# Three block-Winograd stages: combinations of the second input half traced in pieces, and two weight splits queued behind the scaled transposes

## The chip, the cores and the metric

One core of one Trainium2 chip runs the whole program. The metric is the device time of one execution in microseconds, as the median of several runs. The engines are TensorE (PE in the profile; PEld are its weight loads), VectorE (DVE), ScalarE (ACT), GpSimd (POOL) and SyncE (SP), which here issues the plain loads.

## The reference

Two layers work on 512 tokens of width 1024. Each has a token mixer and a squared-ReLU MLP, each behind an RMSNorm and added to the residual.

```
for i in range(DEPTH):                       # DEPTH = 2
    h = rms_norm(x, norm_mix[i])
    x = x + (mla_mixer(h, ...) if i % 2 == 0 else chunked_sgu_mixer(h, ...))
    h = rms_norm(x, norm_ffn[i])
    x = x + jnp.square(jax.nn.relu(h @ w_up[i])) @ w_down[i]    # 1024 -> 4096 -> 1024
return rms_norm(x, final_norm)
# chunked_sgu_mixer: gelu(h @ w_in), 1024 -> 4096; half of it normalised, mixed in chunks and
# used as a gate for the other half; then @ w_out, 2048 -> 1024
```

The change touches the first product of three stages: `h @ w_up` of layer 0 (called FFN0 here), `h @ w_in` (SGU) and `h @ w_up` of layer 1 (FFN1).

## The kernel before

**Arithmetic.** All products are in float32. Each operand is split into two parts of lower precision, high = round(a) and low = a - high, and a product is three matmuls: high by high, high by low, low by high (`mm3`, L110). `split` makes the two parts of a tile: a copy on ACT (L125), then a subtraction on DVE (L122). A tile of weights is 128 x 2048; an input quarter 128 x 1024.

**Seven products for eight.** Large products are taken by a Strassen-Winograd scheme with seven block products. The input, transposed, has four quarters a11, a21 (first half of the columns, ready early) and a12, a22 (second half). The class `Quarters` makes them. `first` turns the first half and gives A11 and S3. `rest` makes what the other five products need: A12; n1 = a22 - a21 and N1; s2 = -n1 - a11 and S2; A22; s4 = -a12 - s2 and S4. Capital names are the splits. `turn` (L312) does a half: four times four transposes on PE into a PSUM bank (L296), then one half of the bank scaled on ACT (L316) and the other on DVE (L317).

**Items.** Each stage is a list `work` of items. An item has `prepare` (fetch or combine the weights, then split them) and `go` (48 matmuls of 256 columns in FFN0 and FFN1, 24 of 512 in the gates of SGU, then the handling of the result). The loops at the end of `ffn` and of the SGU stage prepare two items ahead. In FFN0 and FFN1 the items begin: 0 uses A11, 1 uses S3, 2 uses A12, 3 uses S2, 4 uses N1, 5 uses A22, 6 uses S4. In SGU two such lists run side by side: 0 and 1 use A11, 2 and 3 A12, 4 and 5 N1, 6 and 7 S4, 8 and 9 S2, 10 and 11 S3, 12 and 13 A22.

**Weights.** `load` (L987) is a plain load on SP. `add` (L990) is a load issued by POOL that adds to what the tile holds. In FFN0 and FFN1 item 2 loads a tile of its own ("c"). Item 3's weights are made by `p2` (L1044), a DVE addition of tile "b" to tile "a", followed by the split. Item 4's are "b" after an `add`, which can only start when L1044 has read "b". Item 5's are "a" after another `add`, which can only start when item 3's split has read "a". In SGU the weights of items 2 and 3 pass one after the other through one tile, `W`, so the second load waits for the split of the first.

**Order.** The instructions are traced in the order of the Python code. A scheduler then gives each engine a fixed order: when an engine is free in its own model, it takes the earliest-traced instruction that is ready. So an instruction that is traced late can stand in front of one traced early that still waits. On the chip each engine keeps that order. `tc.issue_after(ins)` puts what a block traces on `ins`'s engine behind `ins`, without waiting for its end; `behind(pair)` does so for two instructions. `wtiles` has three slots for split weights.

**Before the change** `rest` runs as a whole inside `go` of item 0. In FFN0 and FFN1 it writes a12, a22 and n1 into tiles of the pool for the squares. In SGU it writes them into `uq[0]`, the tile u0 whose memory later serves as the slots U1 and U2 for the weights of items 6 and 7.

Of the kernel before, what the change touches and what calls it, by code (L numbers as in the profile page):

```python
# [18 lines left out]
T = 512  # L19
# [38 lines left out]
def trunk(ctx: ExitStack, tc: tile.TileContext, a):  # L58
# [65 lines left out]
    def split(hl, src, eng=None):  # L124
        nc.scalar.copy(hl[0], src)  # L125
        low(eng or nc.vector, hl[1], src, hl[0])
        return hl
# [162 lines left out]
    def four(dtype=F32R):  # L290
        return gxp.tile([P, 4, H], dtype, tag="g", name=nm("g"))
# [7 lines left out]
    class Quarters:  # L299
# [12 lines left out]
        def turn(self, e, lo, hi):  # L312
            for k in range(4):
                kk = self.halves[e] * 4 + k
                ps, g = turned(kk), self.g[kk]
                nc.scalar.activation(lo[:, k, :], ps[:, 0:H], AF.Copy, scale=g)  # L316
                nc.vector.tensor_scalar(  # L317
                    out=hi[:, k, :], in0=ps[:, H:T], scalar1=g, scalar2=None, op0=ALU.mult
                )

        def first(self):
# [6 lines left out]

        def rest(self, a12, a22, n1):

            self.turn(1, a12, a22)
            stt = nc.vector.scalar_tensor_tensor
            nc.vector.tensor_sub(n1, a22, self.a21)
            s2, s4 = self.a11, a12
            stt(out=s2, in0=n1, scalar=-1.0, in1=self.a11, op0=ALU.mult, op1=ALU.subtract)
            self.A12 = split((four(), G6[0]), a12)
            stt(out=s4, in0=a12, scalar=-1.0, in1=s2, op0=ALU.mult, op1=ALU.subtract)
            self.S2 = split((G6[1], G6[2]), s2)
            self.N1 = split((G6[3], G6[4]), n1)
            self.A22 = split((G6[5], four()), a22)  # L340
            self.S4 = split((four(), four()), s4)

# [215 lines left out]
    with tc.tile_pool(name="att", bufs=1) as att:  # L560
# [347 lines left out]
        def after(i, u):  # L908
            norm.add(i, u)
# [3 lines left out]
        def go(n):  # L913
            for _ in range(min(n, len(waiting))):
                waiting.pop(0)()
# [76 lines left out]
    def ffn(layer, xq, norm, pool, after=None, last=None, mid=None):  # L992
# [24 lines left out]
        def up(c):  # L1017

            def w(i, k):
                return wview(w_up, xq.row(k), 512, c * 1024 + i * 512, 512)  # L1020

            s, sq, acc = {}, {}, {}
            X, YZ = banks[0:2], banks[2:4]
            acc = {"X": X, "Y": YZ, "Z": YZ if c else banks[4:6]}

            def fetch(name, i, k):
                s[name] = raws.get()
                load(s[name], w(i, k))

            def w11():  # L1030
                fetch("b", 0, 0)
                return "b"

            def w12():
                fetch("c", 0, 1)
                return "c"

            def p1():
                fetch("a", 1, 0)
                add(s["a"], w(1, 1))  # L1040
                return "a"

            def p2():
                nc.vector.tensor_add(s["a"], s["a"], s["b"])  # L1044
                return "a"

            def p3():
                add(s["b"], w(1, 0))
                return "b"

            def p4():
                add(s["a"], w(0, 1))
                return "a"

            def w22():
                fetch("c", 1, 1)
                return "c"

            def both(name, f):
                if name not in sq:  # L1060
                    sq[name] = squares.get()
                for j in range(2):
                    f(sq[name][:, 2 * j : 2 * j + 2, :], j)

            def pv(ps):
                return ps.rearrange("p (m n) -> p m n", m=2)

            def keep(name, sums):
                both(name, lambda t, j: nc.scalar.copy(t, pv(acc[sums][j])))

            def plus(name, sums):
                both(name, lambda t, j: nc.vector.tensor_add(t, t, pv(acc[sums][j])))  # L1072

            def square(name, scale):
                t = sq[name]
                nc.scalar.activation(t, t, AF.Relu, scale=scale)
                nc.scalar.activation(t, t, AF.Square)

            def end1():
                keep("a11", "X")  # L1080

            def end2():
                plus("a11", "Z")
                square("a11", 1.0)

            def end5():
                keep("a22", "Y")

            def end6():
                keep("a21", "X")  # L1090

            def end7():
                plus("a22", "X")
                square("a22", -1.0)

            def end3():
                plus("a21", "Y")
                square("a21", 1.0)

            def end4():  # L1100
                both("a12", lambda t, j: nc.scalar.activation(
                    t, pv(acc["X"][j]), AF.Relu, scale=-1.0))
                nc.scalar.activation(sq["a12"], sq["a12"], AF.Square)

            def item(weights, right, sums, first, end, free=False):
                ww = []

                def prepare():
                    name = weights()
                    ww.extend(split(wtiles(4, 512, 16), s[name]))  # L1110
                    if free:
                        raws.put(s.pop(name))

                def go():
                    r = getattr(xq, right)
                    for m in range(4):
                        ms = slice(m * P, (m + 1) * P)
                        out = acc[sums][m // 2][:, (m % 2) * H : (m % 2 + 1) * H]
                        for k in range(4):
                            mm3(  # L1120
                                out, (ww[0][:, k, ms], ww[1][:, k, ms]),
                                (r[0][:, k, :], r[1][:, k, :]),
                                first and k == 0 and m % 2 == 0, k == 3, skip_group_check=True,
                            )
                    end()

                return prepare, go

            m1 = item(w11, "A11", "X", True, end1)
            m2 = item(w12, "A12", "Z", True, end2, True)  # L1130
            m5 = item(p1, "S3", "Y", True, end5)
            m6 = item(p2, "S2", "X", False, end6)
            m7 = item(p3, "N1", "X", False, end7, True)
            m3 = item(p4, "A22", "Y", False, end3, True)
            m4 = item(w22, "S4", "X", False, end4, True)
            if c == 0:
                begin = m1[1]

                def first():
                    begin()  # L1140
                    three = [squares.get() for _ in range(3)]
                    xq.rest(*three)
                    for t in three:
                        squares.put(t)
                    nc.vector.reciprocal(r2, norm.mean())
                    nc.vector.tensor_scalar(
                        out=nr2, in0=r2, scalar1=-1.0, scalar2=None, op0=ALU.mult
                    )

                return [(m1[0], first), m5, m2, m6, m7, m3, m4], sq  # L1150
            return [m1, m2, m5, m6, m7, m3, m4], sq

        def accumulate(i, u, ps, r):
# [131 lines left out]
        n_mixed = len(work)  # L1285
        if last is None:
            work += down(3, sq)
        ahead = 2
        for prepare, _ in work[:ahead]:
            prepare()  # L1290
        for j, (_, go) in enumerate(work):
            if j == 1:
                spare[:] = banks[6:8]
            if j == 7:
                spare[:] = []
            if j == n_mixed:
                spare[:] = banks[0:2]
            go()
            if j + ahead < len(work):
                work[j + ahead][0]()  # L1300
        if last is not None:
            spare[:] = banks
            last(
# [24 lines left out]
    with stage(1), tc.tile_pool(name="sgu", bufs=1) as sg:  # L1328
# [378 lines left out]
        def after(n, f):  # L1707
            then.setdefault(n, []).append(f)

        def begin():  # L1710
            gx1.rest(*(uq[0][t] for t in ("a11", "a12", "a21")))
            r = inv_sqrt(norm1.mean())
            with tc.issue_after(root[0].ins):
                mix_load()
            norms["r"], norms["nr"] = r, small()
            nc.vector.tensor_scalar(
                out=norms["nr"], in0=r, scalar1=-1.0, scalar2=None, op0=ALU.mult
            )
# [25 lines left out]
        def banks_are(t):  # L1744
            spare[:] = t

        after(0, begin)
        after(6, lambda: banks_are(E))
        after(8, rows_of_r)
        after(9, lambda: (mix_transposed(0), mix_transposed(1)))  # L1750
# [23 lines left out]
        for j, (_, go) in enumerate(work):  # L1774
            go()
            for f in then.get(j, ()):
                f()
            if j + ahead < len(work):
                work[j + ahead][0]()
        fixed[0] = None  # L1780

# [116 lines left out]
```

## Time and profile before

| | us |
|---|---|
| median of 3 runs | 1098.06 (1094.0 to 1098.29) |
| the profiled execution, its own time | 1092.22 |
| span of its instructions | 1090.5 |
| mean granted clock | 0.989 of full speed |

The three stages begin near 177 us (FFN0), 502 us (SGU) and 763 us (FFN1) of the span. The timeline gives, for each engine, the start of an instruction (or of several alike in a row), how long it lasted, and in brackets how long the engine stood idle before it and what ended that. Busy times of matmuls overlap, as they are pipelined; the distance between starts is the cost of one.

### The profile page before, as it was taken

The numbers are of one execution on the slowest core, as the hardware profiler recorded it, in microseconds if no ns is written. First come the engines' busy times: TensorE is split into PE (matmuls) and PEld (weight loads), VectorE is DVE, ScalarE is ACT, GpSimd is POOL, SyncE is SP. The second block draws the span as 40 slices with busy tenths as digits, with TensorE's granted clock in tenths as the row PEclk, the third lists the DMA queues.
The fourth block names the chain that finished last, engine by engine and source line by source line (L and its number), as shares of the span: only waits on it lengthen the run. The fifth ranks groups of instructions, "written<-read, shape, count | busy, mean of one in ns | idle before, by whom it ended". The sixth has DMA issues, their size and how long they took to land.

```text
span 1090.5 us, 15740 instructions
## 1 busy us (share of the span) xinstructions
PE 1058.8 (97%) x6540; PEld 947.4 (87%) x6540; DVE 864.3 (79%) x959; ACT 627.8 (58%) x712; POOL 115.4 (11%) x143
## 2 busy tenths in 40 slices
PE   8989999899999999989999999999999999999997
PEld 6778889899999999877788999887999899999986
DVE  6888866887887887887968588997988788888753
ACT  4567546665655655556755645556765555656531
POOL 5100000001001001002011000010001001001000
PEclk9989999999999999999999999999999999999999
DMA  6120246768768669447486836876686886757421
GB/s 204 39 79 2 76 117 197 204 142 174 212 144 186 178 149 199 149 78 175 139 161 141 231 85 193 237 134 181 156 222 125 218 194 125 225 115 119 120 109 59
DMA packets 86083, 163.33 MB, mean 150 GB/s; under 512 B 4917, under 2 KB 10620, under 8 KB 85884
## 3 DMA queue, kind: packets, MB, share of 16 engines
q0 software_dynamic: 33584, 67.11, 35.3%
q1 hardware_dynamic: 52428, 95.22, 25.4%
q8 instruction: 51, 0.84, 0.3%
q14 instruction: 20, 0.16, 0.0%
HBM read 160.22 MB, written 2.10 MB: 149 GB/s over the span
## 4 chain that ended last, share of the span: by engine, by line
PE 79%; DVE 8%; DMA 4%; issue 4%; ACT 4%; SPq 0%; POOL 0%; POOLq 0%; ACTq 0%; DVEq 0%
PE ps L110 74%; DVE wl L122 3%; ACT wh L125 2%; DMA wb<-in_sgu_w_in 2%; DMA wb<-in_ffn_w_down 1%; DVE g L122 1%; PE ps L1613 1%; PE ps L852 1%; DMA wb<-in_ffn_w_up 1%; PE ps L296 1%; PE ps L819 0%; PE ps L820 0%; PE ps L821 0%; PE ps L823 0%; PE ps L822 0%
## 5 line engine op out<-in xcount | busy, mean ns | idle before, releaser
L110 PE MATMUL ps<-g,wh 128*128 128x256 f32 (+1 forms) x2304 | 420.5, 285 | 9.0 <-DVE g L122 5.0
L110 PEld LDWEIGHTS ps<-g,wh 128*128 128x128 f32 x2304 | 359.9, 190 | 17.2 <-DVE g L122 5.9
L110 PE MATMUL ps<-g,wl 128*128 128x256 f32 (+1 forms) x1152 | 327.1, 284 | 0.6 <-DVE wl L122 0.6
L110 PE MATMUL ps<-wh,q 128*128 128x512 f32 (+1 forms) x840 | 266.5, 390 | 2.9 <-DVE x L1155 2.9
L122 DVE TENSOR_TENSOR wl<-wb,wh 128x2048 fp32r<-128x2048 f32 x75 | 171.7, 2289 | 68.8 <-ACT wh L125 68.8
L110 PEld LDWEIGHTS ps<-g,wl 128*128 128x128 f32 x1152 | 217.4, 189 | 2.2 <-DVE wl L122 0.9
L125 ACT CAST wh<-wb 128x2048 fp32r<-128x2048 f32 x75 | 143.0, 1907 | 119.5 <-PE ps L110 92.0
L110 PEld LDWEIGHTS ps<-wh,q 128*128 128x128 f32 x840 | 158.1, 189 | 34.9 <-issue 3.3
L122 DVE TENSOR_TENSOR wl<-wr,wh 128x2048 fp32r<-128x2048 f32 (+1 forms) x69 | 153.3, 2225 | 38.5 <-ACT wh L125 38.4
L125 ACT CAST wh<-wr 128x2048 fp32r<-128x2048 f32 (+1 forms) x69 | 127.8, 1855 | 64.2 <-PE ps L110 44.8
L110 PE MATMUL ps<-wl,q 128*128 128x512 f32 (+1 forms) x420 | 163.7, 390 | 0.0
L110 PE MATMUL ps<-wh,g 128*128 128x512 f32 x496 | 157.5, 395 | 1.9 <-DVE g L122 1.3
L110 PEld LDWEIGHTS ps<-wh,g 128*128 128x128 f32 x496 | 93.8, 189 | 23.3 <-DVE g L122 1.7
L125 ACT CAST q<-sq 128x1024 fp32r<-128x1024 f32 x51 | 53.6, 1051 | 90.4 <-PE ps L110 87.8
L110 PE MATMUL ps<-wl,g 128*128 128x512 f32 x248 | 97.7, 394 | 1.7 <-DVE wl L122 1.7
L110 PEld LDWEIGHTS ps<-wl,q 128*128 128x128 f32 x420 | 79.5, 189 | 14.5
L1155 DVE SCALAR_TENSOR_TENSOR x<-ps,s,x 128x512 f32<-128x512 f32 x98 | 72.6, 746 | 20.9 <-PE ps L110 20.9
L122 DVE TENSOR_TENSOR q<-sq,q 128x1024 fp32r<-128x1024 f32 x51 | 62.4, 1223 | 5.3 <-ACT q L125 2.3
L110 PEld LDWEIGHTS ps<-wl,g 128*128 128x128 f32 x248 | 46.9, 189 | 12.5 <-DVE wl L122 2.5
L990 POOL DMA_DIRECT2D wr<-in_ffn_w_up x16 | 20.9, 1308 | 268.9 <-DMA wr<-in_ffn_w_up 84.9
L990 POOL DMA_DIRECT2D wb<-in_ffn_w_down x17 | 21.9, 1291 | 133.8 <-DVE wl L122 131.6
L1072 DVE TENSOR_TENSOR sq<-sq,ps 128x512 f32<-128x512 f32 x48 | 32.6, 681 | 3.9 <-PE ps L110 2.6
(267 smaller groups left out, 1276.2 us busy)
## 6 DMA issues: line engine op xcount, KB each, us to landing
wb<-in_ffn_w_up SPq DMA_DIRECT2D x18, 1024.0 KB, 5.7
wb<-in_ffn_w_down SPq DMA_DIRECT2D x18, 1024.0 KB, 5.1
wb<-in_ffn_w_down POOLq DMA_DIRECT2D x17, 1024.0 KB, 9.4
wr<-in_ffn_w_up POOLq DMA_DIRECT2D x16, 1024.0 KB, 8.5
wr<-in_ffn_w_up SPq DMA_DIRECT2D x14, 1024.0 KB, 5.5
wr<-in_sgu_w_in POOLq DMA_DIRECT2D x9, 1024.0 KB, 10.4
wr<-in_ffn_w_down SPq DMA_DIRECT2D x8, 1024.0 KB, 5.1
wb<-in_ffn_w_up POOLq DMA_DIRECT2D x8, 1024.0 KB, 8.6
```

The source lines that it names most:

```text
L110: nc.tensor.matmul(out, lhsT=lhsT, rhs=rhs, start=start and t == 0, stop=stop and t == 2, **kw)
L122: return eng.tensor_sub(l, src, h.bitcast(F32))
L125: nc.scalar.copy(hl[0], src)
L296: nc.tensor.transpose(ps[:, i * P : (i + 1) * P], x[:, i, k * P : (k + 1) * P], ident)
L852: nc.tensor.transpose(ps[b][:, c : c + P], pr[h, i][:, j * P : (j + 1) * P], ident)
L990: nc.gpsimd.dma_start(t, src, accum_op=ALU.add)
L1072: both(name, lambda t, j: nc.vector.tensor_add(t, t, pv(acc[sums][j])))
L1155: nc.vector.scalar_tensor_tensor(out=xs, in0=ps, scalar=r[:, i : i + 1], in1=xs, op0=ALU.mult, op1=ALU.add)
L1613: nc.tensor.matmul(ps[:, i * P : (i + 1) * P], lhsT=m[:, i, :], rhs=wt[:, j // 2, :], start=True, stop=True,)
```

## The change

It makes `rest` return six functions instead of doing the work, and calls them in the loops after the `go` of certain items:

| piece | FFN0 and FFN1: traced after | SGU: traced after |
|---|---|---|
| `second`: the transposes, scaling, A12 | item 0 | item 0 |
| `difference`: n1 | item 1 | item 0 |
| `sums`: s2, S2 | item 1 | item 3 |
| `negative`: N1 | item 2 | item 0 |
| `both_sums`: s4 | item 3 | item 3 |
| `others`: A22 and S4 | item 3, A22 first | item 3, S4 first |

`turn` keeps its last pair of scalings in `self.ends`, and in all three stages the `prepare` of items 2 and 3 runs inside `behind(...ends)`: all that it traces on ACT and DVE goes behind the last scaling of that engine. In FFN0 and FFN1 the small scalings of the norm move from item 0 to after item 2. In SGU the three tiles are now the two halves of `Bt` and `wt`, which are not filled until items 9 and 10; u0 is no longer used for them.

```diff
+                self.ends = (
+                    nc.scalar.activation(lo[:, k, :], ps[:, 0:H], AF.Copy, scale=g),
+                    nc.vector.tensor_scalar(
+                        out=hi[:, k, :], in0=ps[:, H:T], scalar1=g, scalar2=None, op0=ALU.mult
+                    ),
                 )
...
+            def second():
+                self.turn(1, a12, a22)
+                self.A12 = split((four(), G6[0]), a12)
+            def difference():
+                nc.vector.tensor_sub(n1, a22, self.a21)
+            def sums():
+                stt(out=s2, in0=n1, scalar=-1.0, in1=self.a11, op0=ALU.mult, op1=ALU.subtract)
+                self.S2 = split((G6[1], G6[2]), s2)
+            def negative():
+                self.N1 = split((G6[3], G6[4]), n1)
+            def both_sums():
+                stt(out=s4, in0=a12, scalar=-1.0, in1=s2, op0=ALU.mult, op1=ALU.subtract)
...
+        then = {
+            0: [begin],
+            1: [lambda: three[3][1](), lambda: three[3][2]()],
+            2: [lambda: three[3][3](), scales],
+            3: [others],
+        }
...
             go()
+            for f in then.get(j, ()):
+                f()
             if j + ahead < len(work):
-                work[j + ahead][0]()
+                if j < 2:
+                    with behind(xq.ends):
+                        work[j + ahead][0]()
+                else:
+                    work[j + ahead][0]()
...
+        wide = Bt.rearrange("p (e k a) t -> p e k (a t)", e=2, k=4)
+        rest = gx1.rest(wide[:, 0], wide[:, 1], wt.rearrange("p (k a) t -> p k (a t)", k=4))
+        def combinations():
+            rest[2]()
+            rest[4]()
+            rest[5](("S4", "A22"))
         def begin():
-            gx1.rest(*(uq[0][t] for t in ("a11", "a12", "a21")))
+            rest[0]()
+            rest[1]()
+            rest[3]()
...
+        after(3, combinations)
```

## Rows read from the trace of the kernel before

**Rows 1.** The page, part 1: busy time, share of the span, instructions.
```profile
PE 1058.8 (97%) x6540; PEld 947.4 (87%) x6540; DVE 864.3 (79%) x959; ACT 627.8 (58%) x712; POOL 115.4 (11%) x143
```
**Rows 2.** Timeline of PE, FFN0: start, length, instruction, [idle before, what ended it].
```profile
182.53 1.91 PE L296 MATMUL ps<-ident,x 128*128 128x128 f32 x16
...
189.81 0.28 PE L110 MATMUL ps<-g,wl 128*128 128x256 f32 x1
190.25 0.50 PE L110 MATMUL ps<-g,wh 128*128 128x256 f32 x2 [0.16 <-ACT g L125]
193.92 0.58 PE L110 MATMUL ps<-g,wh 128*128 128x256 f32 x1 [3.16 <-DVE g L122]
```
**Rows 3.** Windows of FFN0: length, each engine's busy time, granted clock, DMA, GB/s.
```profile
189.90:193.90 4.00, 0.70 (x4) 0.30 (x2) 4.00 (x4) 4.00 (x5) 1.28 (x1) 0.97 0.87 320
193.90:197.20 3.30, 3.28 (x15) 3.28 (x16) 3.30 (x4) 2.02 (x3) 0.00 (x0) 0.52 0.98 174
197.20:206.00 8.80, 8.80 (x77) 8.80 (x76) 8.80 (x8) 6.00 (x6) 0.00 (x0) 1.00 0.37 63
```
**Rows 4.** Timeline of DVE, FFN0.
```profile
169.22 2.28 DVE L1044 TENSOR_TENSOR wr<-wr,wr 128x2048 f32<-128x2048 f32 x1
...
185.54 2.29 DVE L122 TENSOR_TENSOR wl<-wb,wh 128x2048 fp32r<-128x2048 f32 x1 [5.95 <-ACT wh L125]
187.75 1.65 DVE L317 TENSOR_SCALAR sq<-ps,G 128x256 f32<-128x256 f32 x4
189.32 2.28 DVE L122 TENSOR_TENSOR wl<-wr,wh 128x2048 fp32r<-128x2048 f32 x1
191.52 1.21 DVE L333 TENSOR_TENSOR sq<-sq,g 128x1024 f32<-128x1024 f32 x1
192.66 1.21 DVE L122 TENSOR_TENSOR g<-sq,g 128x1024 fp32r<-128x1024 f32 x1
```
**Rows 5.** Timeline of ACT, FFN0.
```profile
185.89 1.57 ACT L316 ACTIVATE sq<-ps,G 128x256 f32<-128x256 f32 x4
...
189.12 2.02 ACT L125 CAST g<-sq 128x1024 fp32r<-128x1024 f32 x2
```
**Rows 6.** Timeline of POOL, FFN0: the adding loads of items 4 and 5.
```profile
172.05 1.30 POOL L990 DMA_DIRECT2D wr<-in_ffn_w_up  x1 [18.80 <-ACT g L316]
191.89 1.28 POOL L990 DMA_DIRECT2D wr<-in_ffn_w_up  x1 [18.54 <-DVE wl L122]
```
**Rows 7.** The page, part 6: issues, KB each, median us to landing.
```profile
wr<-in_ffn_w_up POOLq DMA_DIRECT2D x16, 1024.0 KB, 8.5
```
**Rows 8.** Timeline of PE, SGU, items 2 and 3.
```profile
515.44 0.50 PE L110 MATMUL ps<-wh,g 128*128 128x512 f32 x1 [0.46 <-ACT g L125]
...
517.43 0.80 PE L110 MATMUL ps<-wh,g 128*128 128x512 f32 x2 [1.26 <-DVE g L122]
...
526.45 0.50 PE L110 MATMUL ps<-wl,g 128*128 128x512 f32 x1 [1.66 <-DVE wl L122]
```
**Rows 9.** Timelines of SP, ACT and DVE, SGU: loads and splits of tile W.
```profile
501.99 13.08 SPq L987 DMA_DIRECT2D wb<-in_sgu_w_in  x2
...
510.44 1.91 ACT L125 CAST wh<-wb 128x2048 fp32r<-128x2048 f32 x1 [3.94 <-DMA wb<-in_sgu_w_in]
...
520.08 1.90 ACT L125 CAST wh<-wb 128x2048 fp32r<-128x2048 f32 x1 [0.48 <-DMA wb<-in_sgu_w_in]
...
524.11 2.28 DVE L122 TENSOR_TENSOR wl<-wb,wh 128x2048 fp32r<-128x2048 f32 x1
```
**Rows 10.** Timelines of PE and DVE, FFN1.
```profile
770.56 0.60 PE L296 MATMUL ps<-ident,x 128*128 128x128 f32 x4
...
777.63 0.39 PE L110 MATMUL ps<-g,wh 128*128 128x256 f32 x1 [0.78 <-DVE g L122]
...
784.44 0.39 PE L110 MATMUL ps<-g,wh 128*128 128x256 f32 x1 [1.09 <-DVE g L122]
...
760.96 2.28 DVE L1044 TENSOR_TENSOR wr<-wr,wr 128x2048 f32<-128x2048 f32 x1
```

More of the change, by code (lines that the diff above doesn't have):

```diff
@@ L315, in turn @@
                 ps, g = turned(kk), self.g[kk]
-                nc.scalar.activation(lo[:, k, :], ps[:, 0:H], AF.Copy, scale=g)
-                nc.vector.tensor_scalar(
-                    out=hi[:, k, :], in0=ps[:, H:T], scalar1=g, scalar2=None, op0=ALU.mult
+                self.ends = (
[3 more added lines that the diff above has]
+                    ),
                 )
@@ L329, in rest, with others @@
         def rest(self, a12, a22, n1):
-            self.turn(1, a12, a22)
             stt = nc.vector.scalar_tensor_tensor
-            nc.vector.tensor_sub(n1, a22, self.a21)
             s2, s4 = self.a11, a12
[L335 to L341, printed above, removed]
+            def second():
[10 more added lines that the diff above has]
+                stt(out=s4, in0=a12, scalar=-1.0, in1=s2, op0=ALU.mult, op1=ALU.subtract)
+            def others(order):
+                for name in order:
+                    if name == "A22":
+                        self.A22 = split((G6[5], four()), a22)
+                    else:
+                        self.S4 = split((four(), four()), s4)
+            return second, difference, sums, negative, both_sums, others
     wd = a["mla_w_dkv"][0]
@@ L1136, in up @@
             if c == 0:
[L1137 to L1150, printed above, removed]
+                return [m1, m5, m2, m6, m7, m3, m4], sq
             return [m1, m2, m5, m6, m7, m3, m4], sq
@@ L1287, in ffn, with begin, scales, others @@
             work += down(3, sq)
+        three = []
+        def begin():
+            three.extend(squares.get() for _ in range(3))
+            three.append(xq.rest(*three))
+            three[3][0]()
+        def scales():
+            nc.vector.reciprocal(r2, norm.mean())
+            nc.vector.tensor_scalar(out=nr2, in0=r2, scalar1=-1.0, scalar2=None, op0=ALU.mult)
+        def others():
+            three[3][4]()
+            three[3][5](("A22", "S4"))
+            for t in three[:3]:
+                squares.put(t)
+        then = {
[4 more added lines that the diff above has]
+        }
         ahead = 2
@@ L1298, in ffn @@
             go()
+            for f in then.get(j, ()):
+                f()
             if j + ahead < len(work):
-                work[j + ahead][0]()
+                if j < 2:
+                    with behind(xq.ends):
+                        work[j + ahead][0]()
+                else:
+                    work[j + ahead][0]()
         if last is not None:
@@ L1777, in trunk @@
                 f()
-            if j + ahead < len(work):
+            if j < 2:
+                with behind(gx1.ends):
+                    work[j + ahead][0]()
+            elif j + ahead < len(work):
                 work[j + ahead][0]()
```

## The prediction
> **What bounds the kernel now.** Read the engine shares first: PE is busy for 97% of the span [rows 1], so only time in which PE waits, or runs at the lower clock, can be won. Then look for its waits on PE's timeline in the three stages that the change touches.
>
> FFN0: item 1 issues its last matmul at 189.81. Item 2 starts at 190.25, gets two matmuls in, and stands for 3.16 us, with 0.16 us before that, until DVE has written A12's low part [rows 2]. The windows show what follows: 15 matmuls take 3.30 us at a granted clock of 0.52 (the 1.2 GHz level), while 77 take 8.80 us at 1.00 [rows 3], so 0.22 us each against 0.114, and 15 x 0.106 = 1.6 us go as well. FFN0 therefore loses 0.16 + 3.16 + 1.6 = 4.9 us. On DVE the cause stands in order: item 2's weights (185.54), the scalings (187.75), item 3's weights (189.32), n1 (191.52), and only then A12's low part, at 192.66 [rows 4].
>
> FFN1 loses 0.78 us before item 2 and 1.09 us before item 3 [rows 10]: 1.9 us, with no long idle stretch. SGU waits 0.46 and 1.26 us in item 2 and 1.66 us in item 3 [rows 8]. The three stages together hold about 10 us, under 1% of the time. This is all that the change can win.
>
> **The change, part by part: order on DVE and ACT.** The dependent steps are not removed, they are moved. What I use for the new order is the old one: right after the scalings DVE took item 3's weights, which were traced later than n1 but were ready, and n1, which needs the scaling just issued, came second [rows 4]. So behind the last scaling I expect a ready, independent instruction first. Two of those are put there by `behind`. On ACT it is the copy of item 2's weights, ahead of A12's copy. On DVE it is L1044: it belongs to `prepare` of item 3, so the 2.28 us that ran at 169.22 in FFN0 and at 760.96 in FFN1, when DVE had time [rows 4, 10], now fall into the crowded stretch. That is the cost of this change, and it lies on the path.
>
> **FFN0, worked out.** Steps from start to start on DVE: 2.2 us for a weight tile or L1044 (189.32 to 191.52), 1.14 for a quarter (191.52 to 192.66) [rows 4]. The transposes end at 182.53 + 1.91 = 184.44 [rows 2]; the four ACT scalings take 1.57 us in all [rows 5] and the first three overlap the transposes, so the last ends near 184.95, and DVE's last 0.5 later, 185.45. ACT: item 2's copy (1.91, as in SGU [rows 9]) to 186.85, A12's copy (1.0 each by 2.02 for two [rows 5]) to 187.9, item 3's copy to 189.8. DVE: L1044 to 187.65, item 2's low part to 189.85, A12's low part to 191.0. Item 2 can start at 189.93, and its third matmul would be due at 190.15, so it waits 0.9 us instead of 3.3. Then n1 to 192.1, item 3's low part to 194.3, s2 to 195.4, S2's low part to 196.6, or 197.7 if N1's slips in ahead while ACT copies S2. Item 2's other 46 matmuls end at 191.05 + 46 x 0.114 = 196.3, and item 3's third is due at 196.5: it waits 0.1 to 1.2 us. Sum 1.0 to 2.1 lost, against 4.9. **Gain 2.8 to 3.9, taken as 3.4**; the short waits leave the clock at its level.
>
> Who stands behind the moved steps: item 4's adding load follows L1044, so it goes from 172.05 [rows 6] to about 187.9. With 8.5 us to land [rows 7] it is there at 196.4, its split done some 4.2 us later, at 200.7, and item 4 starts near 202.5: hidden, by 1.8 us. Item 5's follows item 3's split, from 191.89 [rows 6] to 194.6, landed 203.1, split 207.3 against a start near 208: hidden by under 1 us, and costing what it overruns if DVE is late. SP's loads are not behind anything new. The norm's scalings, S4 and A22 are needed two items later and cost nothing.
>
> **FFN1, worked out.** Here item 2's and item 3's weights and L1044 were ready before the scalings, so there was less to win. The last four transposes stand behind item 0 (770.56, ending 771.16 [rows 10]); every bank lacks a quarter until then, so all four ACT scalings follow: 771.16 + 1.57 = 772.7, DVE's last at 773.2. Same chain: L1044 775.4, item 2's weights 777.6, A12's low part 778.8. Item 2 could start at 777.63 - 0.78 = 776.85; its third matmul now waits until 778.85, about 2.0 us. Item 3 again waits 0 to 1.1 us. Lost 2.0 to 3.1 against 1.9. **Taken as 0.5 us slower**, between 1.2 slower and, if A12 gets ahead of L1044, 1.0 faster.
>
> **SGU, worked out.** There is no L1044 here, and item 2's wait can go. But item 3 is held by tile W: the first load lands at 510.4, its split takes 1.91 + 2.2, the second load is issued by 501.99 + 13.08 = 515.07, lands at 520.08, is copied by 521.98, and could be subtracted by 522.0 + 2.3 = 524.3; DVE was late and started it at 524.11 [rows 9]. PE's 526.45 [rows 8] can become 524.3 at the best, however early item 2 ends. So 2.1 us is the bound. Item 2 then ends near 521.3, and PE waits some 3 us in item 3, as long as the wait in FFN0 after which the clock fell for 1.6 us [rows 2, 3]; that may be lost again. The weights of items 6 and 7 go to u0, which is free now, so SP issues them right behind W's first load; they can delay W's second by up to the time of their 2 MB at 320 GB/s [rows 3], 6.6 us, if it had to wait for all of it, and by nothing if they are done before 515. They have 12 us for it, so I take 0.6. **Net 0.5 us gained**, between 2.1 gained and 1.7 lost.
>
> The Trainium skill's page "DMA: Bandwidth & Descriptors", section "Issuing engines are not separate DMA queues", says that all transfers run on the same 16 DMA engines and interleave. That speaks against early loads. No row here has these three in flight together. By that rule W's first load would land with the last of them, which is the second rival below; the sum above goes without it.
>
> **Sum.** 3.4 - 0.5 + 0.5 = 3.4 us faster. On the profiled execution (span 1090.5, time 1092.22) that is 1088.8. The runs shown have a median of 1098.06, 5.8 us above that execution, and go down to 1094.0, so the forecast is made as a difference from the median: 1098.06 - 3.4 = 1094.7. About 0.5% (5.5 us) is what a measurement of this kernel can tell from no change.
>
> **The rivals.**
> *All waits go.* If A12's low part and S2's are ahead of L1044 and the weights just in time, FFN0 gives 4.9, FFN1 1.9 and SGU 2.1: 8.9 us, 1089.2. For it: the work per item fits in PE's time for it. Against: DVE needs 9 us from the scalings to S2's low part, and L1044 is in there.
> *Early loads hold W up.* If the 2 MB share the engines with W's first load, it lands up to 6.6 us later and PE's third matmul of item 3 comes at 524.3 + 6.6 = 530.9 instead of 526.45: SGU loses 4.4, the sum is 3.4 - 0.5 - 4.4 = -1.5, 1099.6. Against: W's load is issued first.
> *Nothing is reordered on the path* because the scheduler takes what is ready as before: 1098.1. Against: `behind` does force item 3's weights behind the scalings.
> *L1044 comes last* (slower). If n1, A12, item 2's weights, s2 and S2, all traced earlier, are taken first, L1044 ends in FFN0 near 195.7, item 3's split at 199.8 and item 4's load lands at 204.4, split 208.5. Item 3 waits 4 us and item 4 3.4 us, with the clock falling twice (3.2): 10.7 lost against 4.9, so 5.8 slower; FFN1, with 0.9 us less in hand, 11.7 against 1.9, so 9.8 slower. With SGU's 0.5 gain, 1113. It decides once L1044 ends later than about 190 in FFN0. Against: item 3's weights went ahead of n1 in the old order.
>
> **How the numbers follow.** Forecast 0.42 (its own range 1092 to 1098), all waits go 0.22, early loads 0.12, nothing 0.12, L1044 last 0.12. The range 1088 to 1101 leaves out the last and a little of the first rival, under 0.2. Faster by over 0.5% (below 1092.6): 0.22 and a seventh of the forecast's 0.42, 0.28. Slower by over 0.5% (above 1103.5): 0.12 and a little, 0.14. Within: 0.58.
>
> **What would show it.** Right: on DVE in FFN0 and FFN1 the scalings are followed by L1044, then item 2's weights, then A12; PE's wait before item 2's third matmul in FFN0 shrinks to about 1 us with the clock at 1.00 after it, and grows to about 2 us in FFN1; in SGU item 3's wait stays and ends near 524. Wrong: a wait in item 4 or 5 on a POOL load, W's first load landing after 511, or L1044 behind S2.

## The result, and the profile after

| | before | after |
|---|---|---|
| median of 6 runs, us | 1096.03 (1092.15 to 1102.05) | 1106.13 (1104.63 to 1107.83) |
| ratio, with its 95% interval | | 1.0096 (1.0074 to 1.0117) |
| span of the profiled execution, us | 1090.5 | 1102.9 |

The change makes the kernel 0.96% slower, some 10.5 us; the prediction had 3.4 us faster, with a range that ended at 1101. In the new file the line numbers from the scalings on are higher: L1063 is the addition of b to a (L1044 before), L317 and L318 are the scalings, L341 makes n1, L344 makes s2, L351 makes s4, L1006 is the plain load, L1009 the adding load, and L1088 the copy that takes an item's result out of PSUM.

The page of the kernel after, part 1, shows next to nothing of it; the shares are within one point of those in [rows 1]:
```profile
PE 1063.7 (96%) x6540; PEld 951.3 (86%) x6540; DVE 866.9 (79%) x959; ACT 627.5 (57%) x712; POOL 116.4 (11%) x143
```
The timeline of PE does. First FFN0, then SGU, then FFN1, only the rows with a wait:
```profile
191.10 0.38 PE L110 MATMUL ps<-g,wh 128*128 128x256 f32 x1 [0.73 <-DVE g L122]
201.23 0.80 PE L110 MATMUL ps<-g,wh 128*128 128x256 f32 x2 [4.45 <-ACT g L125]
202.49 0.58 PE L110 MATMUL ps<-g,wh 128*128 128x256 f32 x1 [0.46 <-DVE g L122]
...
519.23 0.73 PE L110 MATMUL ps<-wh,g 128*128 128x512 f32 x2 [0.85 <-DVE g L122]
527.57 0.73 PE L110 MATMUL ps<-wh,g 128*128 128x512 f32 x2 [3.27 <-ACT wh L125]
529.89 0.79 PE L110 MATMUL ps<-wl,g 128*128 128x512 f32 x1 [1.59 <-DVE wl L122]
...
782.84 0.38 PE L110 MATMUL ps<-g,wh 128*128 128x256 f32 x1 [1.05 <-DVE g L122]
793.03 0.80 PE L110 MATMUL ps<-g,wh 128*128 128x256 f32 x2 [4.51 <-ACT g L125]
794.29 0.58 PE L110 MATMUL ps<-g,wh 128*128 128x256 f32 x1 [0.46 <-DVE g L122]
```
In each FFN stage the wait at item 2 (191.10, 782.84) is now short, and item 3 (201.23, 793.03) waits over 4 us. Windows behind these waits (columns as in [rows 3]; FFN0, then FFN1):
```profile
203.00:207.60 4.60, 4.60 (x24) 4.60 (x23) 4.60 (x5) 3.34 (x3) 0.00 (x0) 0.51 0.50 101
207.60:216.00 8.40, 8.40 (x76) 8.40 (x76) 6.46 (x5) 5.65 (x7) 0.00 (x0) 1.00 0.66 223
...
794.80:798.00 3.20, 3.20 (x17) 3.20 (x16) 3.20 (x3) 1.67 (x2) 0.00 (x0) 0.50 0.49 90
798.00:806.00 8.00, 8.00 (x70) 8.00 (x69) 6.72 (x5) 7.01 (x7) 0.00 (x0) 1.00 0.80 248
```
The granted clock of 0.51 is the 1.2 GHz level. A window's count takes in matmuls that only reach over its edges, so the cost is taken from the starts on the timeline: 23 matmuls start from 202.49 on until the spacing is short again at 207.55, 0.220 us each against 0.114 at full clock, so 23 x 0.106 = 2.4 us. In FFN1 17 start from 794.29 to 798.06, 0.222 each: 1.8 us. So FFN0 loses 0.73 + 4.45 + 0.46 + 2.4 = 8.0 us where the kernel before lost 4.9, and FFN1 1.05 + 4.51 + 0.46 + 1.8 = 7.8 against 1.9.

SGU's waits are 0.85 + 3.27 + 1.59 = 5.7 against 0.46 + 1.26 + 1.66 = 3.4 [rows 8]. The clock fell there in both kernels: 11 matmuls of 512 columns took 4.21 us from 517.43 on before the change (granted clock 0.59), and 12 took 5.29 us from 529.89 on after it (0.50), at 0.23 us each at full clock. That costs 1.7 and 2.5 us, so SGU loses 8.2 against 5.1. The three stages together lose 3.1 + 5.9 + 3.1 = 12.1 us more. The two profiled executions that these rows come from differ by 1102.9 - 1090.5 = 12.4 us; the medians of six runs by 10.1.

A second account is the distance on PE's timeline from the first matmul of one stage's item 0 to that of the next, and from FFN1's to PE's last matmul. One profiled execution each:

| us | FFN0 to SGU | SGU to FFN1 | FFN1 to the end |
|---|---|---|---|
| before | 325.1 | 261.4 | 319.9 |
| after | 327.5 | 264.2 | 327.1 |

**Why item 3 waits.** DVE, FFN0:
```profile
183.77 1.74 DVE L318 TENSOR_SCALAR sq<-ps,G 128x256 f32<-128x256 f32 x4 [3.18 <-ACT sq L317]
185.43 2.28 DVE L1063 TENSOR_TENSOR wr<-wr,wr 128x2048 f32<-128x2048 f32 x1
187.63 2.29 DVE L122 TENSOR_TENSOR wl<-wb,wh 128x2048 fp32r<-128x2048 f32 x1
189.83 1.22 DVE L122 TENSOR_TENSOR g<-sq,g 128x1024 fp32r<-128x1024 f32 x1
190.96 1.22 DVE L341 TENSOR_TENSOR sq<-sq,g 128x1024 f32<-128x1024 f32 x1
192.10 2.29 DVE L122 TENSOR_TENSOR wl<-wr,wh 128x2048 fp32r<-128x2048 f32 x1
194.30 1.22 DVE L344 SCALAR_TENSOR_TENSOR g<-sq,g 128x1024 f32<-128x1024 f32 x1
...
201.21 1.22 DVE L122 TENSOR_TENSOR g<-g,g 128x1024 fp32r<-128x1024 f32 x1 [3.96 <-ACT g L125]
```
Against [rows 4] the scalings are now followed by L1063, item 2's weights and A12's low part; s2 is there at 195.5. But S2's low part starts at 201.21, as ACT is late with S2's high part. ACT in the same stretch, then the same place of FFN1:
```profile
192.22 1.05 ACT L125 CAST g<-sq 128x1024 fp32r<-128x1024 f32 x1 [0.77 <-DVE sq L341]
198.34 1.90 ACT L125 CAST wh<-wr 128x2048 fp32r<-128x2048 f32 x1 [5.07 <-DMA wr<-in_ffn_w_up]
200.14 1.04 ACT L125 CAST g<-g 128x1024 fp32r<-128x1024 f32 x1
...
205.31 1.90 ACT L125 CAST wh<-wr 128x2048 fp32r<-128x2048 f32 x1 [1.19 <-DMA wr<-in_ffn_w_up]
...
790.13 1.90 ACT L125 CAST wh<-wr 128x2048 fp32r<-128x2048 f32 x1 [5.13 <-DMA wr<-in_ffn_w_up]
791.94 1.04 ACT L125 CAST g<-g 128x1024 fp32r<-128x1024 f32 x1
```
The copy of item 4's weights stands ahead of S2's copy in ACT's fixed order and waits 5.07 us for its adding load, with ACT idle and s2 ready. Why that load is late, on POOL:
```profile
188.26 1.30 POOL L1009 DMA_DIRECT2D wr<-in_ffn_w_up  x1 [34.30 <-ACT sq L1088]
194.68 1.28 POOL L1009 DMA_DIRECT2D wr<-in_ffn_w_up  x1 [5.12 <-DVE wl L122]
```
Item 4's was issued at 172.05 before, item 5's at 191.89 [rows 6]. Item 4's follows the addition of b to a: in FFN0 it comes 0.55 us after the end of that instruction in both kernels (171.50 to 172.05, 187.71 to 188.26), in FFN1 0.65 us after it in both. The bracket names another instruction, which ended at about the same time and is not the same one in the two kernels.

### The profile page after: what moved, and what is told of

Same layout as the page of the kernel before. It is cut to its first block, busy times and chain, and to the rows that moved or that the text cites. A ratio compares the mean times of both kernels' runs of the same rounds, so it can differ in the third digit from the quotient of the medians.

```text
span 1102.9 us, 15731 instructions
## 1 busy us (share of the span) xinstructions
PE 1063.7 (96%) x6540; PEld 951.3 (86%) x6540; DVE 866.9 (79%) x959; ACT 627.5 (57%) x712; POOL 116.4 (11%) x143
## 4 chain that ended last, share of the span: by engine, by line
PE 79%; DMA 6%; DVE 5%; ACT 4%; issue 4%; SPq 0%; POOL 0%; POOLq 0%; ACTq 0%; DVEq 0%
PE ps L110 74%; DMA wb<-in_sgu_w_in 2%; ACT wh L125 2%; DVE wl L122 2%; DMA wr<-in_ffn_w_up 2%; DMA wb<-in_ffn_w_down 1%; PE ps L1648 1%; PE ps L871 1%; PE ps L296 1%; DVE g L122 0%; PE ps L838 0%; PE ps L839 0%; PE ps L840 0%; PE ps L842 0%; PE ps L841 0%
## 5 line engine op out<-in xcount | busy, mean ns | idle before, releaser
L1009 POOL DMA_DIRECT2D wr<-in_ffn_w_up x16 | 20.9, 1309 | 277.7 <-DMA wr<-in_ffn_w_up 85.1
L1009 POOL DMA_DIRECT2D wb<-in_ffn_w_down x17 | 21.9, 1291 | 134.8 <-DVE wl L122 132.6
```

Source lines behind the costliest of these rows:

```text
L1009: nc.gpsimd.dma_start(t, src, accum_op=ALU.add)
```

## The experiments

The expectations of the first four runs were written with the rows above in view. What the later ones call theory C was formed after the fourth, and is told there. Ratios are to the kernel before on the same chip, with 95% intervals; the experiments were spread over three chips. A stage's distance is the one of the table above, from one profiled execution.

**Which stage.** `e3_ffn_only` has FFN0 and FFN1 as in the change and SGU as before, `e4_sgu_only` the reverse. `rest_before` is the old `rest`, in one piece.
```diff
 # e3: SGU
-            rest[0]()
-            rest[1]()
-            rest[3]()
+            gx1.rest_before(*(uq[0][t] for t in ("a11", "a12", "a21")))
...
-        after(3, combinations)
...
-            if j < 2:
-                with behind(gx1.ends):
-                    work[j + ahead][0]()
-            elif j + ahead < len(work):
+            if j + ahead < len(work):
                 work[j + ahead][0]()
 # e4: the same in ffn
```


> FFN0 and FFN1 as in the changed kernel, SGU as before. Two theories for the FFN stages. A: item 4's copy of its weights stands on ACT in front of S2's copy and waits there for a load that the change made late (198.3 in FFN0, 790.1 in FFN1), so PE stands in item 3 for 4.7 us in each stage and the clock falls after it. B: the trouble is the crowd on DVE behind the scalings. Both expect the larger part of the loss here: by the distances between the starts of the stages in the two traces (FFN0 to SGU 2.4 us longer, FFN1 to the end 7.2 us longer) about 9 us slower than before.

> SGU as in the changed kernel, FFN0 and FFN1 as before. From the start of SGU to the start of FFN1 the changed kernel took 2.8 us more, so 2 to 4 us slower than before, with item 3's first matmul near 1.5 us later after the stage's start than before and the lower clock for some 5 us behind it. If the loss in SGU were a follow-on of the stage ahead, no change.


Measured: FFN alone 1103.42 us, 1.0085 (1.0064 to 1.0107), some 9 us; SGU alone 1095.19 us, 1.0022 (1.0006 to 1.0039), some 2 us, both as expected. Added up that is 1.0107, within the interval of the whole change. So about four fifths lie in the FFN stages.

**The splits behind the scalings, the addition free.** `e1_splits_behind`:
```diff
-                def prepare():
+                def prepare(order=nullcontext):
                     name = weights()
-                    ww.extend(split(wtiles(4, 512, 16), s[name]))
+                    with order():
+                        ww.extend(split(wtiles(4, 512, 16), s[name]))
...
-                    with behind(xq.ends):
-                        work[j + ahead][0]()
+                    work[j + ahead][0](lambda: behind(xq.ends))
```


> The changed kernel, but in FFN0 and FFN1 only the splits of items 2 and 3 go behind the scalings; L1063 (the addition of b to a) is free again. A and B both expect it to run near 169 in FFN0 and 761 in FFN1, and item 4's load to land long before its copy. Then PE's wait in item 3 is under 1 us in both stages and the FFN stages are 4 to 6 us better than before; with SGU still 3 us worse, 1 to 3 us faster than before in all.


Measured: 1091.79 us, 0.9982 (0.9966 to 0.9999). One instruction moved back, L1063, turns the loss of 0.96% into a gain of 0.2%, which is only just clear of noise. POOL, FFN0, then FFN1:
```profile
172.27 1.30 POOL L1009 DMA_DIRECT2D wr<-in_ffn_w_up  x1 [18.01 <-ACT g L317]
...
779.44 1.28 POOL L1009 DMA_DIRECT2D wr<-in_ffn_w_up  x1 [16.83 <-DVE wl L122]
```
and PE's waits in items 2 to 5 of FFN0, and the longest in FFN1:
```profile
191.19 0.50 PE L110 MATMUL ps<-g,wh 128*128 128x256 f32 x2 [0.41 <-ACT wh L125]
208.46 0.38 PE L110 MATMUL ps<-g,wl 128*128 128x256 f32 x1 [0.72 <-DVE wl L122]
...
791.23 0.51 PE L110 MATMUL ps<-g,wh 128*128 128x256 f32 x2 [1.82 <-ACT sq L1088]
```
FFN0 is now nearly free of waits: its distance is 320.3 us, 4.8 less than before. FFN1's is 323.4, 3.5 more, where the two stages together had been expected to gain 4 to 6 us. There item 5's adding load, which follows item 3's split, is issued 18.6 us after the stage's start (760.82); in the kernel before it was 11.9 (775.28 against 763.39). ACT's copy of item 5's weights then waits for it with PSUM copies that PE needs behind it; behind the wait of 1.82 us the granted clock was 0.50 from 792 to 794.

**S2's copy put ahead of item 4's copy on ACT.** `e5_copy_order` is the change with one order more.
```diff
+                self.copied = nc.scalar.copy(G6[1], s2)
+                low(nc.vector, G6[2], s2, G6[1])
...
+                elif j == 2:
+                    with tc.issue_after(xq.copied.ins):
+                        work[j + ahead][0]()
```


> The changed kernel, but in FFN0 and FFN1 item 4's copy is queued on ACT behind S2's copy; L1063 and the load stay as late. This tells A from B. A: S2's copy runs near 195.5 in FFN0, item 3 waits 0.1 to 1.3 us instead of 4.7, item 4 waits under 1 us, no low clock; 7 to 10 us faster than the changed kernel, so within 3 us of before. B: DVE is as crowded as in the changed kernel, so it stays within 2 us of that.


Measured: 1104.94 us, 1.0106 (1.0082 to 1.013). No recovery came, so that S2's place in ACT's order is the whole price falls. PE, FFN0, and under it ACT:
```profile
198.12 0.39 PE L110 MATMUL ps<-g,wh 128*128 128x256 f32 x1 [1.28 <-DVE g L122]
...
208.55 0.79 PE L110 MATMUL ps<-g,wh 128*128 128x256 f32 x2 [4.93 <-ACT sq L1090]
```
```profile
197.78 1.91 ACT L125 CAST wh<-wr 128x2048 fp32r<-128x2048 f32 x1 [1.49 <-DMA wr<-in_ffn_w_up]
...
205.17 1.90 ACT L125 CAST wh<-wr 128x2048 fp32r<-128x2048 f32 x1 [4.53 <-DMA wr<-in_ffn_w_up]
...
207.93 0.56 ACT L1090 COPY sq<-ps 128x512 f32<-128x512 f32 x1
```
The first wait did fall, from 4.45 + 0.46 to 1.28. But the next copy on ACT, of item 5's weights, now waits 4.53 us for item 5's adding load, and behind it stands L1090, which takes item 3's result out of the PSUM bank into which item 4 adds. PE waits 4.93 us for that at 208.55. In FFN1 PE waits 4.86 us in the same way. By its time alone this run would speak for theory B, but the wait of 4.93 us is one for ACT, not for DVE. In the change itself ACT waits only 1.19 us for item 5's load (205.31), as PE has lost its time before. Corrected, the theory (C) is: both adding loads are late, and ACT, which keeps its order, holds whatever stands behind the copies that wait for them.

**The two adding loads left out.** `e10_no_adding_loads`: the order of the instructions as in the change, with item 4's and item 5's loads gone from the first list of both FFN stages, so that their sums of weights are not formed.
```diff
             def p3():
-                add(s["b"], w(1, 0))
+                if c:
+                    add(s["b"], w(1, 0))
 # the same in p4
```


> The change, with the two adding loads of items 4 and 5 left out in the first list of FFN0 and FFN1 (the sums of weights are then not formed: this work is left out). The order of every other instruction is asked for as in the change. Theory C, the time is lost because the addition of b to a, now behind the scalings, releases both adding loads late (188.3 and 194.7 us instead of 172.1 and 191.9 in FFN0) and each then needs 8.5 to 10.5 us, a copy of 1.9 and a subtraction of 2.3 before its item can start: without the loads PE's waits of 4.73 and 4.79 us at item 3 go, and so do the low clock behind them (22 and 15 matmuls that took 0.1 us longer, 2.2 and 1.5 us) and the waits of 5.2 and 5.1 us at item 5 to which they moved when S2's copy was put first. That is 11 to 14 us less than the change: 1092 to 1095. Rival D, VectorE's longer chain ahead of S2 is the price whatever the loads do: PE still waits 3 us or more at item 3 in both stages, and the time stays within 4 us of the change (1102 to 1106).


(The wait that it puts at item 5 is the one at 208.55 above: it is item 4 that stands, for item 5's load.) Measured: 1093.05 us, 0.9974 (0.9961 to 0.9988), 13 us less than the change, as theory C had it; no wait of 3 us is left at item 3, so rival D is out. PE's waits of over 1 us that are left behind item 2, FFN0 and FFN1:
```profile
198.18 0.52 PE L110 MATMUL ps<-g,wh 128*128 128x256 f32 x2 [1.55 <-ACT wh L125]
...
783.85 0.50 PE L110 MATMUL ps<-g,wh 128*128 128x256 f32 x2 [1.55 <-ACT wh L125]
```
L1063 still stands behind the scalings here (184.90), so DVE's longer chain costs little by itself. The run takes 2 MB of transfers away in each stage too, so it alone doesn't tell the wait from the traffic. `e1_splits_behind` keeps them, early, and the next run keeps them late.

**The addition behind the scalings, the splits free.** `e12_addition_behind`, the other half of `e1_splits_behind`:
```diff
+                    with order():
-                    name = weights()
+                        name = weights()
                     ww.extend(split(wtiles(4, 512, 16), s[name]))
```


> The change, but in FFN0 and FFN1 only the addition of b to a is queued behind the scalings; the splits of items 2 and 3 are free. It is the other half of the run that left the addition free. Theory C (the late release of the adding loads is the price): the addition still comes behind the scalings, item 4's load is issued after 187 us in FFN0 instead of at 172, it lands near 198, and PE waits 3 us or more at item 3 or 4 in both stages: 5 to 11 us above the kernel before, ratio 1.005 to 1.010. Rival, the queueing of the splits has a part in the loss: then this run is at most 3 us slower than before, ratio under 1.003.


Measured: 1102.12 us, 1.0071 (1.0047 to 1.0096), in theory C's range. SGU's 0.2% are in it. L1063 alone, put there, makes most of the loss, and in FFN1 all of it: the distance is 327.2, for 327.1 in the change. POOL and then PE, FFN0:
```profile
194.28 1.30 POOL L1009 DMA_DIRECT2D wr<-in_ffn_w_up  x1 [39.50 <-DMA wb<-in_ffn_w_up]
```
```profile
199.99 0.38 PE L110 MATMUL ps<-g,wh 128*128 128x256 f32 x1 [2.82 <-DVE g L122]
208.19 0.50 PE L110 MATMUL ps<-g,wh 128*128 128x256 f32 x2 [2.71 <-ACT sq L1088]
```
The first of the two is DVE's: L1063 ran at 191.44 here, so item 3's split and S2's low part behind it were late. The second is again a PSUM copy behind a copy that waited 6.00 us for item 4's load. In FFN1 the change's own pattern comes back, with item 4's copy on ACT and then PE's wait in item 3 for S2's copy behind it (at 789.70):
```profile
787.90 1.90 ACT L125 CAST wh<-wr 128x2048 fp32r<-128x2048 f32 x1 [5.43 <-DMA wr<-in_ffn_w_up]
790.79 0.79 PE L110 MATMUL ps<-g,wh 128*128 128x256 f32 x2 [4.19 <-ACT g L125]
```

**Pieces alone.** `e7_pieces_only` queues nothing behind the scalings in FFN0 and FFN1.
```diff
-                if j < 2:
-                    with behind(xq.ends):
-                        work[j + ahead][0]()
-                else:
-                    work[j + ahead][0]()
+                work[j + ahead][0]()
```


> The change without anything queued behind the scalings in FFN0 and FFN1 (the combinations are still traced in pieces; SGU is as in the change). Theory C: the adding loads are issued as early as before (172 and about 192 us in FFN0), so no wait for them at items 3 to 5, and the FFN stages are as before or up to 3 us shorter, as n1 and S2 come in the order of use; SGU adds its 2 us. Ratio 0.998 to 1.003. If the pieces by themselves gave FFN0 all of its gain (4.8 us in the run with the splits behind), the ratio is 0.9965 to 0.998; if they cost something, over 1.004.


Measured: 1096.45 us, 1.0026 (1.001 to 1.0042), about what SGU costs. FFN1's distance is 320.0, as before; FFN0's is 327.4, 2.3 more. PE still waits in item 2 of FFN0:
```profile
191.01 0.50 PE L110 MATMUL ps<-g,wh 128*128 128x256 f32 x2 [1.93 <-ACT g L125]
193.56 0.58 PE L110 MATMUL ps<-g,wh 128*128 128x256 f32 x1 [2.05 <-DVE g L122]
```
So the pieces win nothing by themselves, and cost nothing that these intervals can tell, which is some 2 us. FFN0's gain in `e1_splits_behind` needs the splits of items 2 and 3 behind the scalings.

**SGU: the loads of items 6 and 7 behind W's second.** Loads of W and U and the second copy of W in the change, on SP and ACT:
```profile
504.41 0.37 SPq L1006 DMA_DIRECT2D wb<-in_sgu_w_in  x1
504.83 2.50 SPq L1006 DMA_DIRECT2D u<-in_sgu_w_in  x2
517.63 12.61 SPq L1006 DMA_DIRECT2D wb<-in_sgu_w_in  x2
...
525.62 1.90 ACT L125 CAST wh<-wb 128x2048 fp32r<-128x2048 f32 x1 [1.38 <-DMA wb<-in_sgu_w_in]
```
The U loads go out right behind W's first. W's second is issued at 517.63 and copied at 525.62, 8.0 us later. In [rows 9] its issue ended at 515.07, so began (0.37 long, as at 504.41) at 514.70, and the copy came at 520.08, 5.4 us later. `e2_u_loads_later` is the change with
```diff
+                second_w = loaded[0]
+            elif j in (4, 5):
+                with tc.issue_after(second_w.ins):
+                    work[j + ahead][0]()
```


> The change, with SGU's loads of U1 and U2 queued on SP behind W's second load instead of ahead of it. Theory: in the change the two U loads share the transfers with W's second load, which took 8.0 us from issue to landing where the kernel before had 5.3, and PE waited 3.66 us at item 3 in SGU for it. Behind it they cost nothing, as items 6 and 7 start over 20 us later. Expected: W's second load takes 5 to 6.5 us, PE's wait at item 3 falls to about 1 us, and the time is 1.5 to 3.5 us less than the change (about 1103; 7 us above the kernel before). Rival: W's second load is held back by its release (item 2's split) and not by the U loads; then the wait at item 3 stays over 2.5 us and the time is that of the change.


Measured: 1101.77 us, 1.006 (1.0037 to 1.0083), some 4 us better than the change's ratio, though the two intervals overlap a little. SP, then PE's waits at item 3:
```profile
503.26 13.25 SPq L1008 DMA_DIRECT2D wb<-in_sgu_w_in  x2
516.57 1.05 SPq L1008 DMA_DIRECT2D u<-in_sgu_w_in  x2
```
```profile
524.15 0.73 PE L110 MATMUL ps<-wh,g 128*128 128x512 f32 x2 [1.79 <-ACT wh L125]
526.94 0.50 PE L110 MATMUL ps<-wl,g 128*128 128x512 f32 x1 [2.05 <-DVE wl L122]
```
The time moved as expected, the wait only partly: 3.84 us at item 3 for 4.86, where 1 was expected. W's second took 5.5 us from issue to landing, as expected, and ACT copied it at 522.21 without waiting; so the rival, its release, is not what held it. But DVE took its low part only at 524.60, behind splits of quarters. SGU's distance fell by 2.4 us, to 261.8. It is a loose measure: with SGU as before it was 261.4, 263.1 and 262.6 us in three executions, and with SGU as in the change 262.7 to 266.5 in seven.

**The parts that win.** `e8_only_ffn0_splits` has FFN0 as in `e1_splits_behind`, and SGU and FFN1 as before. `e11_ffn0_splits_sgu_u_later` has SGU as in `e2_u_loads_later` besides.
```diff
-            for f in then.get(j, ()):
+            for f in () if layer else then.get(j, ()):
...
-                if j < 2:
+                if j < 2 and not layer:
```


> FFN0 alone is changed: pieces, and only the splits of items 2 and 3 queued behind the scalings, the addition of b to a left free. SGU and FFN1 are as before. In the run with this in both FFN stages, the way from FFN0's start to SGU's was 4.8 us shorter than before, and the way from FFN1's start to the end 3.5 us longer (item 3's split came 4 us later there, and the adding load of item 5 behind it). If stages add up, this kernel is 4 to 5 us faster than before: ratio 0.9955 to 0.9965. Rival: what FFN0 gains is given back in SGU (its weights are the limit, and it starts 5 us earlier); then 0 to 2 us faster, ratio 0.998 to 1.

> As the kernel with FFN0 alone changed, but SGU as in the change and with its U loads behind W's second load; FFN1 is as before. If the U loads are all that the change costs in SGU, SGU is no longer than before and up to 1 us shorter: ratio 0.9945 to 0.9965. If SGU loses for another reason (about 2 us as in the run with SGU alone changed): ratio 0.997 to 0.998.


Measured: 1088.66 us, 0.9939 (0.9923 to 0.9954), and 1089.35 us, 0.9954 (0.9932 to 0.9975). The first is 6.7 us faster than the kernel before, more than the 4 to 5 expected; FFN0's distance is 319.8 (5.4 less), FFN1's 320.0. The gain is not given back in SGU. With the U loads late, SGU's part of the change neither wins nor loses anything that these intervals can tell. (SGU's distance in the second run is 266.2, in the slowest of its seven executions, so it settles nothing.)

## Why the prediction was wrong

**The chain on DVE was right.** In FFN0, from the scalings to s2, every step came within 0.2 us of the sum: L1063's successor at 187.63 for 187.65, n1 at 190.96 for 191.0, item 3's low part at 192.10 for 192.1. Item 2's wait in FFN0 was 0.73 for 0.9 and the clock stayed up behind it. In FFN1 it was 1.05 for 2.0: the sum had the scalings end 9.8 us after the stage's start, and they ended after 8.6 (777.16 against 768.57).

**The step that failed** is "hidden, by 1.8 us" for item 4's adding load, and with it "by under 1 us" for item 5's. Each load was weighed against the start of its own item, as if nothing but that item waited for it. For item 3 the sum had a wait of 0.1 to 1.2 us; it was 4.45 + 0.46. Three things were wrong:
- *Who waits.* The copy of those weights is an instruction of ACT, and ACT keeps its order. S2's copy, due at 195.5, stood behind it until 200.14. The prediction's path to S2's low part (196.6 to 197.7) named ACT's copy of S2, but gave it no wait; it ran from 201.21 to 202.43. The section on the kernel before had said that each engine keeps its order, and the prediction had named who stands behind the moved addition on POOL, but not who stands behind the copy on ACT, one step further. `e5_copy_order` shows that this place is not the only one: with it mended no time came back, as the next copy on ACT did the same to item 3's PSUM copy.
- *The load's time.* 8.5 us was the page's median [rows 7]. The two in FFN0 took 10 to 10.5 us from issue to landing, while a plain load of 1 MB was in flight beside the first. An estimate of its part: with the load in at 196.4, as in the sum, the copy of 1.8 us would have let S2's copy start at 198.2, still 2.7 us late of the 4.6 (200.14 - 195.5); the other 1.9 come from the load's lateness against the sum. The prediction's "SP's loads are not behind anything new" was wrong too: that plain load follows item 2's low part on DVE in both kernels (issued at 187.86 before, at 189.94 now). The DMA view of the kernel after, 186 to 206 us (issues, KB each, median us to landing):
```profile
wr<-in_ffn_w_up POOLq DMA_DIRECT2D x2, 1024.0 KB, 10.3
wb<-in_ffn_w_up SPq DMA_DIRECT2D x1, 1024.0 KB, 9.8
```
- *The clock.* Waits of 4.45 and 4.51 us were followed by the lower level for 5.1 and 3.8 us, 2.4 and 1.8 us of loss, in stages where none was counted. Nor do short waits always leave the clock alone, as the sum had it: in SGU before the change it fell behind waits of 0.46 and 1.26 us, while behind 0.78 and 1.09 in FFN1 the granted clock stayed at 1.00. So the "about 10 us" that the three stages were said to hold missed the 1.7 us of SGU.

The Trainium skill's page "Perfetto Trace Analysis", section "Tensor Engine Instruction (MATMUL, LD_WEIGHTS)", says that ACT, DVE and GPSIMD are strict FIFO. The rows agree: ACT idle for 5.07 us at 198.34 with S2's copy ready behind.

**FFN0** was put at 3.4 us faster and became 3.1 slower by its waits and its clock. The 4.9 us were there to be had: by the stage's distance `e1_splits_behind` and `e8_only_ffn0_splits` took 4.8 and 5.4. **FFN1**, put at 0.5 slower, became 5.9 slower by the same mechanism.

**SGU**, put at 0.5 faster, was some 2 us slower by `e4_sgu_only`. Its failed term is the U loads' effect on W's second load, "so I take 0.6" between 0 and 6.6: it was 2.6 (8.0 against 5.4 us), and the wait of over 3 us that it left was followed by the lower clock, which the text had named. W's first load, which the rival "early loads hold W up" had charged, was copied at 513.36, 9.0 us after its issue, against 8.45 in [rows 9]. So that rival had the right cause at the wrong load. The rule on shared DMA engines cited with it agrees with W's second load here. What the prediction drew from it, that W's first load would land with the last of the three, did not come: it took 8.9 us to land, the U loads 14.4.

**The rivals.** "L1044 comes last" and "early loads hold W up" had the right sign. The condition of the first was not met (L1063 ended at 187.7, not later than 190), but a part of it, item 4's load arriving late with a fall of the clock, is what happened at a milder delay. What the text had listed as a sign of being wrong, a wait on a POOL load in item 4 or 5, came one item earlier, through ACT.

**Left open.** How much of the wait for the loads is their late release and how much their longer flight was not separated. By rows it is 16.2 us of later issue against 1.6 us of longer flight for item 4 (198.34 - 188.26 - 8.5), and 2.8 against 2.1 for item 5. The distance from FFN1's start to the end grew by 7.2 us, 1.3 more than its waits and clock account for; that rest was not traced. That the change's SGU as a whole costs more than the U loads was not settled either.

## What to carry to other kernels

When an instruction that frees a buffer is moved behind other work, follow the buffer to the load that it releases, on to the first instruction that waits for that load, and then list everything behind that instruction on its own engine; the price is the wait of the earliest of those that the critical engine needs, not of the item that the load serves, and if that one is moved, of the next. A moved block should be cut finer than the source line that holds it: in FFN0 the splits belonged behind the scalings and the addition, in the same call, did not. With the addition left free in both FFN stages the ratio went from 1.0096 to 0.9982; FFN1 was best left as it was. And put loads that are needed late behind the one that is needed next, even if their buffers are free.

## What was not expected of the hardware

Transfers in flight together took longer, by more than was allowed for: an adding load of 1 MB took 8.5 us as the median over the kernel before and 10.3 beside a plain one, and the plain one took 9.8 beside it; W's second load took 8.0 us with 2 MB issued ahead of it on SP, 5.4 in the kernel before and 5.5 with those 2 MB behind it. In `e12_addition_behind`, whose first adding load was issued at 194.28, 1.0 us before the plain load beside it landed, ACT took up item 4's weights at 202.61, 8.3 us after the issue.
